# Score products of two heads on the two halves of the matmul array's rows, in a decoder trunk with sparse attention

## The chip, the cores and the metric

One core of a Trainium2 chip runs the whole program. The metric is the device time of one execution in microseconds; a lower one is better. The core's engines run side by side: PE (TensorE, matrix products into the eight PSUM banks), PEld (its weight loads), DVE (VectorE), ACT (ScalarE), POOL (GpSimd) and SP, which here issues nearly all DMAs.

## The reference

Two layers over 512 tokens of width 1024. Each is half a SwiGLU step, a mixer, and half a SwiGLU step. In the mixer, 16 heads of width 64 in 2 key groups attend in three branches; the change touches the scores, `q` times keys:

```python
q = (q * q_scale).reshape(B, T, N_KV_GROUPS, HEADS_PER_GROUP, HEAD_DIM)
# compressed keys (31 of them)
s = einsum('bqghd,bngd->bghqn', qc, k_cmp) - slopes * dist_c
o_cmp = einsum('bghqn,bngd->bqghd', masked_softmax(s, dist_c >= 0), v_cmp)
# selected blocks (all 8 blocks are selected) and the sliding window of 512 keys
s = einsum(qc, ks) - slopes * dist_s;  o_slc = masked_softmax(s, dist_s >= 0) @ vs
s = einsum(qc, kw) - slopes * dist_w;  o_win = masked_softmax(s, mask_w) @ vw
o_nsa = gates[0] * o_cmp + gates[1] * o_slc + gates[2] * o_win
merged = g_pool * (o_pool @ w_branch_pool) + g_attn * (o_nsa @ w_branch_nsa)
x = x + merged @ w_out
```

## The kernel before, in words

Activations lie transposed: a tile has 128 features by 512 tokens. Float32 accuracy comes from splitting each operand into a rounded high part and the rest (`split`, L113: ACT copies, DVE subtracts) and summing three products, high by high, high by low, low by high (`mm3`, L117). Weights come through SP in blocks of 1 MB (`load`, L95), are split a step ahead of use, and each unit of a projection is 24 products of 512 columns (`proj`, L126).

The program is written as a list of steps (`run_steps`, L279); within them nobody writes an engine's order out. A planner takes all instructions with their program order as priority and lays each engine's queue down when the program is built: an instruction goes in when its operands and a free buffer of its tag are there in the plan, and a later one that is ready goes ahead of one that isn't. So the products of projections, transposes and heads stand mixed in PE's queue.

PSUM has eight banks of 512 columns by tag (L34): `mm` 2, `sc` 2, `pt` 3, `pv` 1. The attention of a layer runs over 16 heads:

- `query_unit` (L562) makes the queries of two heads. Each head gets a tile of its own, `q`: its 64 rows hold the high part, the other 64 rows the low part. The keys `KH` hold the high part twice, once in each half; `KL` the low part. So one product of 128 rows gives high by high plus low by high, and a second with `KL` gives high by low (L645, L655): two products a bank.
- `cmp_probs` (L576), once for four heads, scores the 31 compressed keys: eight products of 128 rows (L584) into one `sc` bank.
- `head_probs` (L619): for each of four blocks of 128 queries and each of two branches, the scores of all keys up to the block (128 to 512 columns); DVE adds the distance and takes the minimum (L634), ACT takes the exponential (L636), DVE scales by gate over sum (L660 to L664). In blocks 0 and 1 both branches share a bank; in blocks 2 and 3 each has its own, so a head fills six `sc` banks.
- `head_out` (L666): 20 transposes a head into six `pt` banks (L677), each bank split (ACT, DVE), then 17 products with the values into `pv` (L691); the sum of its halves goes to `o` (L695), a tile in SBUF that holds all heads.

Head h's probabilities are written ahead of head h-1's outputs, and between heads stand "fill" units, the gate projections and later queries (L749). After head 15 `split_out` (L765) splits `o` for the next projection, `branch_nsa` (L783).

Of the kernel before, what the change touches and what calls it, by code (L numbers as in the profile page):

```python
# [17 lines left out]
P = 128  # L18
# [12 lines left out]
OFF_KC, OFF_KS, OFF_KW, OFF_GATE = 1024, 1280, 1536, 1792  # L31
OFF_POOL, OFF_GP, OFF_GA = 1840, 2352, 3376
SLOPES = [float(np.float32(2.0 ** (-(h + 1) / 2))) for h in range(H)]
BANKS = {"mm": 2, "sc": 2, "pt": 3, "pv": 1}  # L34
FF_CHUNKS = ((0, 8), (8, 8), (16, 6))

ROWS = {"ffn1_norm": 0, "mix_norm": 16, "ffn2_norm": 32, "final_norm": 48,
# [14 lines left out]
class Trunk:  # L52
# [416 lines left out]
    def compress_out(self, w2, hid, which):  # L469
        nc = self.nc  # L470
        hs = self.s("hs")[:62, :256]
        nc.scalar.activation(hs, hid[64:126, :256], AF.Copy)
        nc.vector.tensor_add(hs, hid[:62, :256], hs)
        nc.scalar.activation(hs, hs, AF.Gelu_apprx_tanh)
        tp = self.bank("pt")
        for c in range(2):
            nc.tensor.transpose(tp[:, c * 62 : c * 62 + 62], hs[:, c * P : c * P + P],
                                self.ident[:62, :62])
        w2r = self.s("w2r")[:, :128].rearrange("p (c d) -> p c d", c=2)
        nc.sync.dma_start(w2r, w2.rearrange("(c p) d -> p c d", p=P))  # L480
        w2h, w2l = self.pr("w2h"), self.pr("w2l")
        if which == 0:
            hh, hl = self.pr("hh")[:, :124], self.pr("hl")[:, :124]
            self.split(hh, hl, tp[:, :124])
            w2h, w2l = (w[:, :256].rearrange("p (c r d) -> p c r d", c=2, r=2)
                        for w in (w2h, w2l))
            self.split(w2h, w2l, bc(w2r, 2, 2))
            kp = self.bank("pv")
            self.mm3(kp[:, :62], [
                (w2h[:, c].rearrange("p r d -> p (r d)"), w2l[:, c].rearrange("p r d -> p (r d)"),  # L490
                 hh[:, c * 62 : c * 62 + 62], hl[:, c * 62 : c * 62 + 62]) for c in range(2)])
            self.Kc = []
            for g in range(G):
                kc = self.unit("Kc", 2, F32R, "Kc", (P, 2, 224))
                nc.gpsimd.memset(f32(kc), 0.0)
                self.split(kc[:, 0, 96:127], kc[:, 1, 96:127], kp[:, g * NCMP : g * NCMP + NCMP])
                self.Kc.append(kc)
            return
        hh, hl = (self.pr(n).rearrange("p (a j n) -> p a j n", a=4, j=4) for n in ("hh", "hl"))
        nc.gpsimd.memset(f32(hh), 0.0)  # L500
        nc.gpsimd.memset(f32(hl), 0.0)
        src = bc(tp[:, :124].rearrange("p (a n) -> p a n", a=4), 2, 4)
        for a in range(4):
            self.split(hh[:, a, :, :NCMP], hl[:, a, :, :NCMP], src[:, a])
        w2h, w2l = (w[:, :128].rearrange("p (c d) -> p c d", c=2) for w in (w2h, w2l))
        self.split(w2h, w2l, w2r)
        self.Vc = []
        for g in range(G):
            vp = self.bank("pv")
            self.mm3(vp[:, :DH], [  # L510
                (hh[:, 2 * c + g].rearrange("p j n -> p (j n)"),
                 hl[:, 2 * c + g].rearrange("p j n -> p (j n)"), w2h[:, c], w2l[:, c])
                for c in range(2)])
            vm = self.s("vm")[:, :128].rearrange("p (j d) -> p j d", j=2)
            nc.vector.tensor_mul(vm, bc(vp[:, :DH], 1, 2), bc(self.block, 2, DH))
            vc = self.unit("Vc", 2, F32R, "Vc", (P, 2, 2, DH))
            self.split(vc[:, :, 0], vc[:, :, 1], vm)
            self.Vc.append(vc)
# [43 lines left out]
    def query_unit(self, m, w):  # L562


        nc = self.nc
        p = self.proj("mm", w, self.xg)
        qn = self.s("qn")
        nc.vector.scalar_tensor_tensor(qn, p, self.qcol[:, m : m + 1], self.R, ALU.mult, ALU.mult)
        for e in range(2):
            q = self.unit("x", 8, F32R, "q")  # L570
            me, other = slice(e * DH, e * DH + DH), slice(DH - e * DH, 2 * DH - e * DH)
            nc.scalar.activation(q[me], qn[me], AF.Copy)
            nc.vector.tensor_sub(q[other], qn[me], f32(q[me]))
            self.qs[2 * m + e] = q

    def cmp_probs(self, qd):  # L576

# [1 line left out]
        nc = self.nc  # L579
        kc = self.Kc[qd // 2]  # L580
        sp = self.bank("sc")
        for j in range(4):
            for part in range(2):
                nc.tensor.matmul(sp, kc[:, part, 96 - 32 * j : 224 - 32 * j], self.qs[4 * qd + j],  # L584
                                 start=j + part == 0, stop=j == 3 and part == 1)
        st = self.s("st")
        nc.vector.tensor_add(st, sp, self.distc)
        tp = self.bank("pt")
# [27 lines left out]
            nc.vector.tensor_sub(pc[other], tp[me], f32(pc[me]))  # L616
            self.pc[qd].append(pc)

    def head_probs(self, h):  # L619

        nc = self.nc
        g, q = h // 8, self.qs.pop(h)
        m, c = self.sm(8, "m"), self.sm(8, "c")
        probs = self.probs[h] = {}

        def slot():
            i = self.tpos % 16
            self.tpos += 1  # L630
            return self.tbuf[i // 8][:, i % 8]

        def softmax_num(t, sp, i, nk):
            nc.vector.tensor_tensor_reduce(t, sp, self.dist[:, T - nk :], SLOPES[h], 3e38,  # L634
                                           ALU.add, ALU.min, m[:, i : i + 1])
            nc.scalar.activation(t, t, AF.Exp, scale=-1.0, bias=m[:, i : i + 1],  # L636
                                 accum_out=c[:, i : i + 1])

        for qb in range(TB):
            nk = P * (qb + 1)  # L640
            qq = q[:, qb * P : qb * P + P]
            if qb < 2:
                sp = self.bank("sc")[:, : 2 * nk]
                for i, K in enumerate((self.KH[g], self.KL[g])):
                    nc.tensor.matmul(sp, qq, K[:, :, :nk], start=i == 0, stop=i == 1)  # L645
                t2 = slot()[:, : 2 * nk].rearrange("p (r k) -> p r k", r=2)
                s2 = sp.rearrange("p (r k) -> p r k", r=2)
                for br in range(2):
                    softmax_num(t2[:, br], s2[:, br], 2 * qb + br, nk)
                    probs[qb, br] = t2[:, br]  # L650
            else:
                for br in range(2):
                    sp = self.bank("sc")[:, :nk]
                    for i, K in enumerate((self.KH[g], self.KL[g])):
                        nc.tensor.matmul(sp, qq, K[:, br, :nk], start=i == 0, stop=i == 1)  # L655
                    t = slot()[:, :nk]
                    softmax_num(t, sp, 2 * qb + br, nk)
                    probs[qb, br] = t
            ci = c[:, 2 * qb : 2 * qb + 2]
            nc.vector.reciprocal(ci, ci)  # L660
            nc.vector.tensor_mul(ci, ci, self.gates[:, qb, 3 * h + 1 : 3 * h + 3])
            for br in range(2):
                t = probs[qb, br]
                nc.vector.tensor_scalar(t, t, ci[:, br : br + 1], None, ALU.mult)  # L664

    def head_out(self, h):  # L666
        nc = self.nc
# [24 lines left out]
        tmp = self.s("otmp")  # L692
        nc.scalar.activation(tmp[:DH], out[DH:], AF.Copy)
        r = (h % 2) * DH
        nc.vector.tensor_add(self.o[r : r + DH, h // 2], out[:DH], tmp[:DH])  # L695


    def mixer(self, l, on_x):
# [3 lines left out]
        def scratch(name):  # L702
            return self.dr.tile([ND, P, T], F32, tag=f"{name}{l}", name=f"{name}{l}")

        dx, dP, dB, dA = (scratch(n) for n in ("dx", "dP", "dB", "dA"))
        self.dx[l] = dx
        self.qs, self.pc, self.probs, self.delta = {}, {}, {}, {}

# [33 lines left out]
                  bp[2]]  # L742

        def start():
            self.tbuf, self.tpos = [self.big(F32, "tbuf") for _ in range(2)], 0
            self.o = self.big(F32, "o")

        steps += [bp[3], (None, start)]
        fill = [gp[0:1] + q[2:3], gp[1:2] + q[3:4], gp[2:3], gp[3:4],  # L749
# [3 lines left out]
        for h in range(H):  # L753
            if h % 4 == 0:
                steps.append((None, lambda h=h: self.cmp_probs(h // 4)))
            steps.append((None, lambda h=h: self.head_probs(h)))
            if h:
                steps.append((None, lambda h=h: self.head_out(h - 1)))
            steps += fill[h]
        steps.append((None, lambda: self.head_out(H - 1)))  # L760

        oh, merged, streams, nx = [], [], {}, [None] * ND
        box = {}
# [1 line left out]
        def split_out():  # L765
            for k in range(ND):
                hi, lo = self.unit("xg", 16, F32R, "oh"), self.unit("xg", 16, F32R, "ol")
                self.split(hi, lo, self.o[:, k])
                oh.append((hi, lo))
            box["mh"], box["ml"] = self.big(F32R, "mh"), self.big(F32R, "ml")  # L770

# [39 lines left out]
    def run(self):  # L811
# [13 lines left out]
        self.x, self.xg = [], []  # L825
        tps = []
        for d in range(ND):
            tp = self.bank(("mm", "sc", "pt", "mm", "sc", "pt", "pt", "pv")[d])
            for tb in range(TB):
                nc.tensor.transpose(tp[:, tb * P : tb * P + P],  # L830
                                    xin[:, tb, d * P : d * P + P], self.ident)
            self.xg.append(self.gain(tp, ROWS["ffn1_norm"] + d))
            tps.append(tp)
# [81 lines left out]
```

## Time and profile before

| | |
|---|---|
| median of 3 runs | 2397.09 us (2396.93 to 2399.38) |
| profiled execution | 2397.52 us, span 2395.7 us |
| granted TensorE clock over the span | 0.995 |
| busy: DVE, ACT, POOL | 1398.9, 977.4, 51.5 us |
| matmuls | 11042 |
| HBM | 101 GB/s over the span |

The span runs from the first to the last instruction; the execution's time has 1.8 us around it. Busy time of PE counts records that overlap, so the room that a product takes is read from the start of one to the start of the next.

### The profile page before, as it was taken

To read this page: it belongs to the slowest core of one execution; us is meant where nothing else is said; L and a number is where in the kernel's file an instruction comes from. 1 tells how busy PE (TensorE), PEld (TensorE's weight loads), DVE (VectorE), ACT (ScalarE), POOL (GpSimd) and SP (SyncE) were. 2 spreads that over 40 slices of the span, in tenths; PEclk is the share of its full clock that TensorE was granted. 3 is DMA by queue.
4 is the path that set the end of the run, shared out by engine and by line. 5 is a ranking of instruction groups with operands and counts; after the bars stand their busy time and mean duration, and the time that the engine had idled before them with its cause. 6 is when DMAs were issued, how large, how long until landed. Compare 5 with 4: busy or idle time off the path is not lost.

```text
span 2395.7 us, 28552 instructions
## 1 busy us (share of the span) xinstructions
PE 2363.0 (99%) x11042; PEld 1955.6 (82%) x11042; DVE 1398.9 (58%) x2684; ACT 977.4 (41%) x1689; POOL 51.5 (2%) x106
## 2 busy tenths in 40 slices
PE   8999999999999999999999999999999999999998
PEld 6888888778888888888888888887888887888887
DVE  4434346768988544443544443567988975434444
ACT  4222235556666432222332222345666664322222
POOL 1000000000001000000000000000000010000000
PEclk9999999999999999999999999999999999999999
DMA  5323224522124432323223232334222253232321
GB/s 159 104 90 105 89 97 140 158 82 62 58 76 153 138 105 89 101 93 101 92 89 105 89 105 90 119 115 156 71 71 80 71 185 110 88 106 88 106 79 62
DMA packets 226007, 244.24 MB, mean 102 GB/s; under 512 B 8688, under 2 KB 206416, under 8 KB 225872
## 3 DMA queue, kind: packets, MB, share of 16 engines
q1 hardware_dynamic: 225696, 242.37, 31.6%
q8 instruction: 87, 1.43, 0.3%
q14 instruction: 48, 0.39, 0.1%
q10 hardware_dynamic: 176, 0.05, 0.0%
HBM read 223.53 MB, written 18.87 MB: 101 GB/s over the span
## 4 chain that ended last, share of the span: by engine, by line
PE 58%; issue 15%; DVE 1%; POOL 1%; ACT 0%; DMA 0%; POOLq 0%; DVEq 0%; ACTq 0%; SPq 0%
PE ps_mm L122 9%; PE ps_mm L121 9%; PE ps_mm L123 9%; PE ps_pv L691 4%; PE ps_sc L121 3%; PE ps_sc L123 3%; PE ps_sc L122 3%; PE ps_pt L121 3%; PE ps_pt L122 3%; PE ps_pt L123 3%; PE ps_pt L677 3%; PE ps_sc L655 2%; PE ps_sc L645 1%; PE ps_sc L584 0%; DMA bP<-dB 0%
## 5 line engine op out<-in xcount | busy, mean ns | idle before, releaser
L114 ACT ACTIVATE wh<-wr 128x1024 fp32r<-128x1024 f32 (+1 forms) x392 | 408.8, 1043 | 1082.5 <-PE ps_mm L122 399.8
L115 DVE TENSOR_TENSOR wl<-wr,wh 128x1024 fp32r<-128x1024 f32 (+1 forms) x392 | 470.1, 1200 | 78.8 <-ACT wh L114 77.3
L121 PE MATMUL ps_sc<-xh,wh 128*128 128x512 f32 x704 | 276.8, 393 | 2.2 <-ACT x L840 2.2
L123 PE MATMUL ps_sc<-xh,wl 128*128 128x512 f32 x704 | 274.7, 390 | 0.0
L122 PE MATMUL ps_sc<-xl,wh 128*128 128x512 f32 x704 | 274.4, 390 | 0.0
L122 PE MATMUL ps_mm<-act,wh 128*128 128x512 f32 x704 | 274.4, 390 | 0.0
L123 PE MATMUL ps_mm<-act,wl 128*128 128x512 f32 x704 | 273.9, 389 | 0.0
L121 PE MATMUL ps_pt<-xh,wh 128*128 128x512 f32 x704 | 273.9, 389 | 0.0
L122 PE MATMUL ps_pt<-xl,wh 128*128 128x512 f32 x704 | 273.9, 389 | 0.0
L123 PE MATMUL ps_pt<-xh,wl 128*128 128x512 f32 x704 | 273.9, 389 | 0.0
L121 PE MATMUL ps_mm<-act,wh 128*128 128x512 f32 x704 | 273.3, 389 | 0.0
L342 DVE SCALAR_TENSOR_TENSOR x<-ps_mm,x 128x512 f32<-128x512 f32 x96 | 66.4, 692 | 239.7 <-PE ps_mm L123 239.7
L333 DVE TENSOR_TENSOR u<-ps_pt,R 128x512 f32<-128x512 f32 x88 | 60.9, 692 | 245.6 <-PE ps_pt L123 245.6
L121 PE MATMUL ps_mm<-xh,wh 128*128 128x512 f32 x512 | 203.2, 397 | 0.0
L325 DVE TENSOR_TENSOR z<-ps_sc,R 128x512 f32<-128x512 f32 x88 | 60.9, 692 | 242.7 <-PE ps_sc L123 242.6
L123 PE MATMUL ps_mm<-xh,wl 128*128 128x512 f32 x512 | 200.8, 392 | 0.0
L122 PE MATMUL ps_mm<-xl,wh 128*128 128x512 f32 x512 | 200.6, 392 | 0.0
L121 PEld LDWEIGHTS ps_sc<-xh,wh 128*128 128x128 f32 x704 | 132.6, 188 | 30.9 <-ACT x L840 2.6
L636 ACT ACTIVATE tbuf<-tbuf,m 128x128 f32<-128x128 f32 (+3 forms) x256 | 142.2, 556 | 36.2 <-DVE m L634 28.3
L122 PEld LDWEIGHTS ps_sc<-xl,wh 128*128 128x128 f32 x704 | 132.6, 188 | 28.1 <-issue 1.0
L122 PEld LDWEIGHTS ps_mm<-act,wh 128*128 128x128 f32 x704 | 132.2, 188 | 28.5 <-DVE act L115 1.3
L123 PEld LDWEIGHTS ps_sc<-xh,wl 128*128 128x128 f32 x704 | 132.5, 188 | 27.9
(238 smaller groups left out, 3870.7 us busy)
## 6 DMA issues: line engine op xcount, KB each, us to landing
wr<-in_ffn_w_gate_dram SPq DMA_DIRECT2D x44, 1024.0 KB, 5.3
wr<-in_ffn_w_up_dram SPq DMA_DIRECT2D x44, 1024.0 KB, 5.3
wr<-in_w_in_dram SPq DMA_DIRECT2D x34, 1024.0 KB, 5.2
wr<-in_ffn_w_down_dram SPq DMA_DIRECT2D x32, 1024.0 KB, 4.9
wr<-in_ffn_w_down_dram SPq DMA_DIRECT2D x16, 768.0 KB, 4.2
wr<-in_w_branch_nsa_dram SPq DMA_DIRECT2D x8, 1024.0 KB, 5.3
wr<-in_w_out_dram SPq DMA_DIRECT2D x8, 1024.0 KB, 5.3
dx<-x SPq DMA_DIRECT2D x16, 256.0 KB, 2.8
```

Source lines behind the costliest of these rows:

```text
L114: self.nc.scalar.activation(hi, src, AF.Copy)
L115: self.nc.vector.tensor_sub(lo, src, f32(hi))
L121: self.nc.tensor.matmul(out, lh, rh, start=first and i == 0, stop=False)
L122: self.nc.tensor.matmul(out, lh, rl, start=False, stop=False)
L123: self.nc.tensor.matmul(out, ll, rh, start=False, stop=last and i == n - 1)
L325: nc.vector.tensor_mul(z, g, self.R)
L333: nc.vector.tensor_mul(u, up, self.R)
L342: nc.vector.scalar_tensor_tensor(x, o, 0.5, x, ALU.mult, ALU.add)
L636: nc.scalar.activation(t, t, AF.Exp, scale=-1.0, bias=m[:, i : i + 1], accum_out=c[:, i : i + 1])
L655: nc.tensor.matmul(sp, qq, K[:, br, :nk], start=i == 0, stop=i == 1)
L677: nc.tensor.transpose(tp[:, w : w + P], probs[qb, br][:, kb * P : kb * P + P], self.ident)
L691: nc.tensor.matmul(out[:, T - n :], lhsT, rhs, start=i == 0, stop=i == len(ops) - 1)
```

## The change

The two heads of a pair keep their places: head 2m in rows 0 to 63, head 2m+1 in rows 64 to 127 of one high tile and one low tile. The scores of each head are three products of 64 rows, the two heads' written alternately into two `sc` banks. `sc` gets three banks, `pt` two. Probabilities of a pair are made together and scaled at the pair's end (`pair_probs`), into three tiles in place of two; the heads' outputs run one pair behind. As `o` has no room any more, each pair's outputs go to DRAM (`dO`) and `split_out` reads them back, except the last pair's.

```diff
-BANKS = {"mm": 2, "sc": 2, "pt": 3, "pv": 1}
+BANKS = {"mm": 2, "sc": 3, "pt": 2, "pv": 1}
...
-                kc = self.unit("Kc", 2, F32R, "Kc", (P, 2, 224))
+                kc = self.unit("Kc", 2, F32R, "Kc", (P, 2, 192))
...
-                self.split(kc[:, 0, 96:127], kc[:, 1, 96:127], kp[:, g * NCMP : g * NCMP + NCMP])
+                for e in range(2):
+                    rows, c = slice(e * DH, e * DH + DH), 64 + 32 * e
+                    self.split(kc[rows, 0, c : c + NCMP], kc[rows, 1, c : c + NCMP],
+                               kp[rows, g * NCMP : g * NCMP + NCMP])
...
-        for e in range(2):
-            q = self.unit("x", 8, F32R, "q")
-            me, other = slice(e * DH, e * DH + DH), slice(DH - e * DH, 2 * DH - e * DH)
-            nc.scalar.activation(q[me], qn[me], AF.Copy)
-            nc.vector.tensor_sub(q[other], qn[me], f32(q[me]))
-            self.qs[2 * m + e] = q
+        qh, ql = (self.unit("x", 8, F32R, n) for n in ("qh", "ql"))
+        self.split(qh, ql, qn)
+        self.qs[m] = qh, ql
...
-        for j in range(4):
-            for part in range(2):
-                nc.tensor.matmul(sp, kc[:, part, 96 - 32 * j : 224 - 32 * j], self.qs[4 * qd + j],
-                                 start=j + part == 0, stop=j == 3 and part == 1)
+        self.mm3(sp, [(kc[:, 0, 64 - 64 * e : 192 - 64 * e], kc[:, 1, 64 - 64 * e : 192 - 64 * e],
+                       *self.qs[2 * qd + e]) for e in range(2)])
...
+    def pair_probs(self, m):
...
+        def scores(qb, brs):
+            nk = P * (qb + 1)
+            sps = [self.bank("sc")[:, : len(brs) * nk].rearrange("p (r k) -> p r k", r=len(brs))
+                   for _ in range(2)]
+            for i, (q, K) in enumerate(((qh, KH), (qh, KL), (ql, KH))):
+                for j, sp in enumerate(sps):
+                    rows = slice(j * DH, j * DH + DH)
+                    nc.tensor.matmul(sp, q[rows, qb * P : qb * P + P],
+                                     K[rows, brs[0] : brs[-1] + 1, :nk], start=i == 0, stop=i == 2)
+            for r, br in enumerate(brs):
+                i = 2 * qb + br
+                for (h, probs, mi, c), sp in zip(heads, sps):
+                    t = probs[qb, br]
+                    nc.vector.tensor_tensor_reduce(t, sp[:, r], self.dist[:, T - nk :], SLOPES[h],
+                                                   3e38, ALU.add, ALU.min, mi[:, i : i + 1])
+                    nc.scalar.activation(t, t, AF.Exp, scale=-1.0, bias=mi[:, i : i + 1],
+                                         accum_out=c[:, i : i + 1])
         for qb in range(TB):
...
+            for brs in ((0, 1),) if qb < 2 else ((0,), (1,)):
+                scores(qb, brs)
+        for h, probs, _, c in heads:
+            nc.vector.reciprocal(c, c)
+            c3 = c.rearrange("p (b r) -> p b r", r=2)
+            nc.vector.tensor_mul(c3, c3, self.gates[:, :, 3 * h + 1 : 3 * h + 3])
+            for (qb, br), t in probs.items():
+                i = 2 * qb + br
+                nc.vector.tensor_scalar(t, t, c[:, i : i + 1], None, ALU.mult)
...
-        nc.vector.tensor_add(self.o[r : r + DH, h // 2], out[:DH], tmp[:DH])
+        if r == 0:
+            self.o = self.s("o")
+        nc.vector.tensor_add(self.o[r : r + DH], out[:DH], tmp[:DH])
+        if r and h < H - 1:
+            nc.sync.dma_start(self.dO[h // 2], self.o)
...
-            steps.append((None, lambda h=h: self.head_probs(h)))
-            if h:
-                steps.append((None, lambda h=h: self.head_out(h - 1)))
+            if h % 2 == 0:
+                steps.append((None, lambda h=h: self.pair_probs(h // 2)))
+            if h > 1:
+                steps.append((None, lambda h=h: self.head_out(h - 2)))
             steps += fill[h]
-        steps.append((None, lambda: self.head_out(H - 1)))
+        for h in (H - 2, H - 1):
+            steps.append((None, lambda h=h: self.head_out(h)))
...
-                self.split(hi, lo, self.o[:, k])
+                o = self.o
+                if k < ND - 1:
+                    o = self.unit("x", 8, F32, "ob")
+                    nc.sync.dma_start(o, dO[k])
+                self.split(hi, lo, o)
```

## Rows read from the trace of the kernel before

**Rows 1.** The page's busy times: us (share of the span) and instructions.

```profile
PE 2363.0 (99%) x11042; PEld 1955.6 (82%) x11042; DVE 1398.9 (58%) x2684; ACT 977.4 (41%) x1689; POOL 51.5 (2%) x106
```

**Rows 2.** Windows: length, busy us by engine (instructions), clock, DMA share, GB/s.

```profile
622.00:690.00 68.00, 67.71 (x361) 56.06 (x361) 60.12 (x185) 43.75 (x109) 1.05 (x1) 1.00 0.25 78
```

**Rows 3.** Waits of PE's loads, 555 to 757 us: total us, times, longest.

```profile
PEld ps_pv L691 <- ACT ph L114: 2.3, 8, 0.4
```

**Rows 4.** Groups by form: busy us, mean ns | idle before.

```profile
L655 PE MATMUL ps_sc<-KH,q 128*128 128x512 f32 x64 | 25.7, 402 | 0.0
```

**Rows 5.** Timeline of PE, 557 to 587 us: start, us, what.

```profile
557.39 2.04 PE L584 MATMUL ps_sc<-q,Kc 128*128 128x512 f32 x8
...
579.39 0.28 PE L645 MATMUL ps_sc<-KH,q 128*128 128x256 f32 x1
...
579.62 0.40 PE L645 MATMUL ps_sc<-KH,q 128*128 128x512 f32 x1
...
582.41 0.33 PE L655 MATMUL ps_sc<-KH,q 128*128 128x384 f32 x1
...
582.76 0.39 PE L121 MATMUL ps_mm<-xh,wh 128*128 128x512 f32 x1
...
584.61 0.34 PE L655 MATMUL ps_sc<-KH,q 128*128 128x384 f32 x1
...
585.19 0.39 PE L655 MATMUL ps_sc<-KH,q 128*128 128x512 f32 x1
...
585.65 0.39 PE L121 MATMUL ps_mm<-xh,wh 128*128 128x512 f32 x1
...
586.11 0.39 PE L655 MATMUL ps_sc<-KH,q 128*128 128x512 f32 x1
```

**Rows 6.** Timeline, 460 to 461.4 us, around the transposes of L477.

```profile
460.20 0.42 ACT L474 ACTIVATE hs<-hs 62x256 f32<-62x256 f32 x1
...
460.44 0.39 PE L122 MATMUL ps_mm<-xl,wh 128*128 128x512 f32 x1
460.76 0.20 PEld L477 LDWEIGHTS ps_pt<-ident,hs 62*128 62x128 f32 x2 [0.35 <-ACT hs L474]
...
461.03 0.50 PE L123 MATMUL ps_mm<-xh,wl 128*128 128x512 f32 x1
...
461.36 0.40 PE L121 MATMUL ps_mm<-xh,wh 128*128 128x512 f32 x1
```

**Rows 7.** Timeline, 580.7 to 581.4 us: a load that waits for ACT.

```profile
580.72 0.60 ACT L114 ACTIVATE ph<-ps_pt 128x512 fp32r<-128x512 f32 x1
...
581.37 0.19 PEld L691 LDWEIGHTS ps_pv<-ph,V 128*128 128x128 f32 x1 [0.27 <-ACT ph L114]
```

**Rows 8.** Timeline, 28.0 to 28.9 us, around a transpose of 80 rows.

```profile
28.07 0.39 PE L122 MATMUL ps_sc<-xl,wh 128*128 128x512 f32 x1
...
28.53 0.23 PE L169 MATMUL ps_pv<-ident,rows 80*128 80x80 f32 x1
...
28.87 0.39 PE L122 MATMUL ps_sc<-xl,wh 128*128 128x512 f32 x1
```

**Rows 9.** Timeline of PE, 385 to 386.1 us: products of two columns.

```profile
385.20 0.95 PE L243 MATMUL ps_pv<-ones,acc 128*128 128x2 f32 x8
386.01 0.49 PE L121 MATMUL ps_mm<-xh,wh 128*128 128x512 f32 x1
```

**Rows 10.** Groups by form on DVE, over the span.

```profile
L634 DVE CUSTOM_DVE_ANT_0 tbuf<-ps_sc,dist 128x512 f32<-128x512 f32 x64 | 43.5, 680 | 0.5
...
L661 DVE TENSOR_TENSOR c<-c,gates 128x2 f32<-128x2 f32 x128 | 22.3, 174 | 0.1
...
L660 DVE RECIPROCAL c<-c 128x2 f32<-128x2 f32 x128 | 20.5, 160 | 1.6 <-ACT tbuf L636 1.0
```

**Rows 11.** DMA issues (KB each, median us to landing), and a product near the attention's end.

```profile
dA<-z SPq DMA_DIRECT2D x16, 256.0 KB, 4.3
...
748.64 0.48 PE L121 MATMUL ps_mm<-oh,wh 128*128 128x512 f32 x1
```

More of the change, by code (lines that the diff above doesn't have):

```diff
@@ L617, in cmp_probs @@
             self.pc[qd].append(pc)
-    def head_probs(self, h):
+    def pair_probs(self, m):
         nc = self.nc
[L624 to L637, printed above, removed]
-        for qb in range(TB):
[L640 to L664, printed above, removed]
@@ new lines, in pair_probs @@
+        g, (qh, ql) = m // 4, self.qs.pop(m)
+        KH, KL = self.KH[g], self.KL[g]
+        heads = []
+        for j in range(2):
+            h = 2 * m + j
+            probs = self.probs[h] = {}
+            heads.append((h, probs, self.sm(8, "m"), self.sm(8, "c")))
+            for br in range(2):
+                i = 4 * (m % 2) + 2 * j + br
+                chunk = self.tbuf[i // 3][:, i % 3 * 1280 : i % 3 * 1280 + 1280]
+                w = 0
+                for qb in range(TB):
+                    probs[qb, br] = chunk[:, w : w + P * (qb + 1)]
+                    w += P * (qb + 1)
@@ L703, in scratch @@
             return self.dr.tile([ND, P, T], F32, tag=f"{name}{l}", name=f"{name}{l}")
-        dx, dP, dB, dA = (scratch(n) for n in ("dx", "dP", "dB", "dA"))
+        dx, dP, dB, dA, dO = (scratch(n) for n in ("dx", "dP", "dB", "dA", "dO"))
         self.dx[l] = dx
@@ L744, in start @@
         def start():
-            self.tbuf, self.tpos = [self.big(F32, "tbuf") for _ in range(2)], 0
-            self.o = self.big(F32, "o")
+            self.tbuf = [self.big(F32, "tbuf").rearrange("p k t -> p (k t)") for _ in range(3)]
+            self.dO = dO
         steps += [bp[3], (None, start)]
@@ L827, in run @@
         for d in range(ND):
-            tp = self.bank(("mm", "sc", "pt", "mm", "sc", "pt", "pt", "pv")[d])
+            tp = self.bank(("mm", "sc", "pt", "mm", "sc", "pt", "sc", "pv")[d])
             for tb in range(TB):
```

## The prediction

> **What bounds the kernel now.** I read the page's busy times first: the matmul engine is busy for 99% of the span, the next engine for 58% [rows 1]. A stage could still hide another limit, so I cut the attention (about 487 to 757 us, and 1665 to 1936 us in the second layer) into stretches of four heads: there PE is busy for 67.71 of 68 us at full clock, DVE for 60.12 [rows 2]. Busy matmul records overlap, so I then asked what PE's weight loads wait for: over 202 us of attention the longest entry of any engine is 2.3 us [rows 3]. Last I read starts instead of durations from the timeline, because a product's record (402 ns, [rows 4]) is longer than the room it takes: two products of 256 columns take 0.23 us from start to start (579.39 to 579.62), two of 384 take 0.35, two of 512 take 0.46 [rows 5]. So PE streams without a pause here. A microsecond taken from PE's stream is a microsecond of the kernel, and one added is one lost; DVE and ACT have 8 us and more of air in 68.
>
> **The score products.** A head has 12 of them: two of 256 columns, two of 512, four of 384, four of 512. By the spacings above that is 0.23 + 0.46 + 0.70 + 0.92 = 2.31 us, 4.62 us for two heads, 73.9 us for the 16 pairs of both layers. After the change a pair has 36 products of 64 rows with the same column counts, three where one head had two, in 12 bank fillings. The trace of before has no two products side by side on halves of the array, so this is bounded from both sides:
> - One after another: 4.62 x 1.5 = 6.93 us a pair, +37.0 us over 16 pairs.
> - Fully side by side: 3.46 us a pair, -18.5 us.
> - Side by side, but each product with a weight load of its own: eight products of only 2 columns take 0.81 us [rows 9], so a load costs some 0.10 us whatever it multiplies, and two of them 0.21 us, more than a pair of 256 (0.115) or 384 columns (0.175) streams. Then 3 x 0.21 + 3 x 0.23 + 6 x 0.21 + 6 x 0.23 = 3.96 us a pair, -10.5 us.
>
> Which bound holds depends on whether the two halves' products stand next to each other in PE's order. The code writes them alternately, but the order is a planner's: in before each refill of a score bank becomes a run of its own as the bank comes free (579.39, 582.41, 584.61, 585.19 and 586.11 for one head, [rows 5]), with other products between. After the change a filling needs two of three banks. The first finds two free, the next finds one: its first half can go at once, its partner waits until DVE has emptied another. DVE empties one 512-column bank in 0.68 us [rows 10], while the three products of a half take 3 x 0.23 = 0.69 us, so a partner comes late about as often as not. I take half of the products beside their partner: (3.96 + 6.93) / 2 = 5.45 us a pair, +13.2 us; -18.5 and +37.0 are kept for the range.
>
> **Changing between 128 and 64 rows.** The one place of before where PE leaves the 128-row form for 64 or fewer are the two 62-row transposes of L477. They begin 0.32 us after the product ahead of them instead of 0.23, and not for want of data: ACT's tile is ready at 460.62 and the load starts at 460.76, 0.14 us later [rows 6], where a load that really waits for ACT starts 0.05 us after it (580.72 + 0.60, then 581.37, [rows 7]). Behind them the next weights are loaded only when they have ended. From 460.44 to 461.36 it is 0.92 us, 0.46 more than the two 512-column products in it need. A transpose of 80 rows, with no change of form, adds 0.80 - 3 x 0.23 = 0.11 us [rows 8]; two would add 0.22 to 0.24. So the change there and back costs 0.46 - 0.24 = 0.22 us at least, and 0.40 if the two transposes are charged only for their 62 columns. All four places of the trace show the same 0.92. I take the middle, 0.31 us for every run of 64-row products, since a run of score products streams longer than its later loads but pays for the first load and the one after it.
>
> Runs: 6 a pair if all six products of a filling stand together, 12 if each bank is a run. I take 8 (some fillings join, half are split): 128 runs x 0.31 = +39.7 us; the ends are 96 x 0.22 = 21 and 192 x 0.40 = 77 us.
>
> The Trainium skill (TensorE: Matmul & The Clock Gate, Part 3: Packing small matmuls) speaks for the change: products on different row groups run concurrently, a few ns apart, 3.07 times as fast for four groups. By it alone the sum would be that of full overlap, which is the first rival below; no run here shows it.
>
> **Compressed scores.** L584 drops from eight 512-column products to six in each of 8 stages. Eight take 0.235 us each [rows 5]: 16 x 0.235 = -3.8 us. They keep 128 rows.
>
> **Edits that I cost at nothing.** The reciprocal and the gate product now run once a head, not four times: 192 instructions of some 0.17 us [rows 10] leave DVE, and the queries are split in one piece, not two. DVE is not what PE waits for: in the view of [rows 3] the loads wait some 5 us of 202 for DVE and ACT, 14 us over both layers, and PE streams on during most of it. So this gives 0 to -14 us; I take 0. The halves of the compressed keys add some small ACT and DVE instructions well ahead of their use. The transposes lose one of three banks; other products fill in as they do for the scores: 0, at most half of one 0.68 us evacuation a head [rows 10], +11. Probabilities are now scaled at a pair's end, one pair ahead of their transposes; the cover is the fill products. Head outputs leave through SP by 14 stores and come back by 14 loads of 256 KB. A store of that size lands in 4.3 us [rows 11], and two heads lie between the last store and its use, some 9 us of PE (2 x 5632 value columns at 0.23 us per 512, 40 transposes of at least 0.10); uncovered it would be about 7 us a layer. SP waits there only behind issues for later weights. At the tail two heads are left after the last fill instead of one; the next stage's products are already mixed in there (748.64 us, [rows 11]), so 0, at most one head's six splits of 0.68 us, +4 us a layer.
>
> **Sum.** +13.2 + 39.7 - 3.8 = +49.1 us. The profiled execution took 2397.5 us (span 2395.7 and 1.8 around it), 0.4 above the median of the runs; on the median that gives 2446 us.
>
> **Rivals.**
> - *Faster: the halves overlap and the change of form is nearly free.* Then -10.5 to -18.5 - 3.8: 2375 to 2383 us, say 2379. For it: PE is the bound, so saved columns count in full. Against it: the four L477 places. It decides only if a run's price, with 96 runs, falls below (10.5 + 3.8) / 96 = 0.15 us (0.23 with full overlap).
> - *Six together.* Every filling's products stay alternate and overlap, but pay 96 x 0.31 = 29.8: +29.8 - 3.8 - 10.5 to 18.5 gives 2405 to 2413 us. For it: the order written in the code. Against it: one free bank lets one half start alone.
> - *The halves never overlap, so the change does not do what its words say.* +37.0 + 39.7 - 3.8 = +72.9: 2470 us; with the ends for the runs 2451 to 2507. For it: no overlap in the trace. Against it: nothing in the trace either.
>
> **How the numbers follow.** Forecast 0.40 (own range 2420 to 2470), faster rival 0.15, six together 0.23, no overlap 0.22. About 0.2% (5 us) is what a measurement of this kernel can tell from no change. Of the faster rival 0.14 is beyond that; 0.06 (the low end of six together, the high end of the first) is within; 0.80 is slower. The range 2390 to 2490 leaves out most of the faster rival and the top of the last.
>
> **What would show it.** In the changed trace: partner products starting a few ns apart or 0.23 us apart; the number of runs of 64-row products, 96 to 192; the step into a run (0.32 against 0.23 us) and a load that starts only after the run; the attention of a layer some 25 us longer while the FFN stages keep their length. Were runs entered at 0.23 us with loads ahead, the main term would be wrong; a long wait of the branch products for reloaded outputs, or PE idle behind DVE, would be a cost that I left out.

## The result and the profile after

The changed kernel takes 2482.88 us (median of 4 runs, 2480.55 to 2487.14) against 2397.43: a ratio of 1.0361, interval 1.0349 to 1.0374. It is slower by 85 us where the sum gave 49. The profiled execution took 2480.73 us, its span is 2478.8 us, 83.1 longer than before, at a granted clock of 0.992.

PE is still the busy engine, with 176 more products; DVE and ACT have less to do than in [rows 1]:

```profile
PE 2431.8 (98%) x11218; PEld 1953.8 (79%) x11218; DVE 1380.6 (56%) x2480; ACT 963.2 (39%) x1677; POOL 50.9 (2%) x106
```

The windows of the two attentions and the one of [rows 2] (length, then busy us of PE, PEld, DVE, ACT, POOL, clock, DMA share, GB/s) show something new: PE is busy for 65.44 of 68 us where it was for 67.71, and in the two attentions it stands for 9 us each.

```profile
487.00:834.00 347.00, 338.11 (x1683) 251.11 (x1683) 252.94 (x657) 193.44 (x467) 14.88 (x13) 1.00 0.29 95
1707.00:2059.00 352.00, 343.08 (x1683) 255.05 (x1683) 252.35 (x657) 192.79 (x466) 14.37 (x11) 0.98 0.28 94
622.00:690.00 68.00, 65.44 (x331) 46.98 (x330) 48.54 (x128) 36.53 (x96) 1.05 (x1) 1.00 0.24 78
```

What PE's loads wait for, in the stretch of [rows 3] (total us, times, longest): the value products waited 2.3 us for ACT's copies of the transposes, now 15.1, up to 1.3 at a time. The transposes' wait for DVE (1.2 before) and the score loads' wait at the line `issue`, on the step into a run (2.1 before), have grown as well.

```profile
PEld ps_pv L692 <- ACT ph L114: 15.1, 33, 1.3
PEld ps_sc L645 <- issue: 8.6, 33, 0.4
...
PEld ps_pt L678 <- DVE pl L115: 3.9, 10, 0.5
```

The timeline of PE around one whole filling and one half filling, to be read by starts as [rows 5]:

```profile
556.96 0.39 PE L123 MATMUL ps_sc<-qh,Kc 128*128 128x512 f32 x1
557.28 0.39 PE L645 MATMUL ps_sc<-KH,qh 64*128 64x256 f32 x2
557.50 0.28 PE L645 MATMUL ps_sc<-KL,qh 64*128 64x256 f32 x2
557.62 0.28 PE L645 MATMUL ps_sc<-KH,ql 64*128 64x256 f32 x2
557.82 0.50 PE L121 MATMUL ps_mm<-xh,wh 128*128 128x512 f32 x1
558.16 0.40 PE L122 MATMUL ps_mm<-xl,wh 128*128 128x512 f32 x1
...
559.40 0.50 PE L645 MATMUL ps_sc<-KH,qh 64*128 64x512 f32 x1
559.75 0.40 PE L645 MATMUL ps_sc<-KL,qh 64*128 64x512 f32 x1
559.99 0.39 PE L645 MATMUL ps_sc<-KH,ql 64*128 64x512 f32 x1
560.31 0.50 PE L122 MATMUL ps_mm<-xl,wh 128*128 128x512 f32 x1
```

The `x2` are partners on the two halves; these start 3 to 4 ns apart. Into the run goes 0.32 us (556.96 to 557.28) where a product of 512 columns makes room after 0.23. The second step inside is long too (0.22 for 256 columns, then 0.12; 0.35 for 512, then 0.24), so is the last (559.99 to 560.31, 0.32) and the first product behind (557.82 to 558.16, 0.34): about 0.1 us at each of four places. The whole trace has 116 runs of such products, and 174 of 460 products inside runs start sooner behind the one ahead than three quarters of the time that the columns of the one ahead take (I call these early starts).

And this is what the pauses look like, in the same layer, all engines:

```profile
587.97 0.45 PE L692 MATMUL ps_pv<-pc,Vc 128*128 128x512 f32 x1
...
588.25 0.60 PE L678 MATMUL ps_pt<-ident,tbuf 128*128 128x128 f32 x4
...
589.07 0.60 ACT L114 ACTIVATE ph<-ps_pt 128x512 fp32r<-128x512 f32 x1
589.08 0.68 DVE L698 TENSOR_TENSOR o<-ps_pv,otmp 64x512 f32<-64x512 f32 x1 [0.21 <-ACT otmp L694]
...
589.68 0.67 DVE L721 TENSOR_TENSOR z<-ps_mm,R 128x512 f32<-128x512 f32 x1
...
589.91 0.47 PE L692 MATMUL ps_pv<-ph,V 128*128 128x512 f32 x1 [1.05 <-DVE o L698]
...
590.41 0.50 PE L121 MATMUL ps_mm<-xh,wh 128*128 128x512 f32 x1
```

PE has written four transposes (588.25), and the value products that use them stand next in its queue: they wait for ACT's copy (`ph`, ready at 589.67) and for the one `pv` bank, which DVE's sum `o` frees at 589.76. A projection's product comes only at 590.41, when DVE has read `z` out of an `mm` bank. Nothing else stands in the queue to be mixed in, and PE stands for a microsecond. With two transpose banks PE writes few transposes ahead of the value products that use them, so the copy in between comes late; that the banks are the cause is argued here and tried below.

To put sizes on this I measured every start-to-start step of PE from the first compressed product to the last product before the output projection, charged 227 ns for 512 columns (less in proportion) and 109 ns for a transpose, and kept score stretches, with the longer steps into and behind a run, apart from all other pauses. In the kernels with scores of 128 rows the score column is the plain charge; pauses at their score steps stand under other pauses. Us per layer, first and second layer (one number where both agree):

| kernel | attention | scores and runs | other pauses |
|---|---|---|---|
| before | 308.8, 306.9 | 36.3 | 18.0, 16.1 |
| changed | 346.1, 351.2 | 68.5 | 25.1, 30.1 |
| rows64_alone | 336.4, 334.5 | 71.0 | 10.9, 9.1 |
| banks_2_3 | 333.5, 335.2 | 70.5 | 10.5, 12.1 |
| same_half | 344.9, 346.6 | 82.2 | 10.0, 11.7 |
| six_together | 335.9, 335.9 | 56.0 | 27.3, 27.2 |
| pairs_128 | 346.6, 346.9 | 36.3 | 55.8, 56.1 |
| pairs_128_banks_2_3 | 316.7, 319.0 | 36.3 | 25.9, 28.2 |
| before_banks_3_2 | 318.9, 317.6 | 36.3 | 28.1, 26.8 |

Before to changed: scores and runs +64.4 over both layers, compressed scores -3.6, other pauses +21.1, together +82 of the 83 us. The split depends on the column for 128 rows: in the kernel before, the steps of score products, into them and behind them, already hold 6.4 us of pauses a layer. With every step at a score counted as such in both kernels it is 42.8 against 71.1 us a layer, so +57 for scores and runs and +29 for other pauses (22 to 50 over both layers).

### The profile page after: what moved, and what is told of

Same layout as the page of the kernel before. It is cut to its first block, busy times and chain, and to the rows that moved or that the text cites. A ratio compares the mean times of both kernels' runs of the same rounds, so it can differ in the third digit from the quotient of the medians.

```text
span 2478.8 us, 28755 instructions
## 1 busy us (share of the span) xinstructions
PE 2431.8 (98%) x11218; PEld 1953.8 (79%) x11218; DVE 1380.6 (56%) x2480; ACT 963.2 (39%) x1677; POOL 50.9 (2%) x106
## 4 chain that ended last, share of the span: by engine, by line
PE 78%; issue 15%; DVE 3%; ACT 1%; DMA 1%; POOL 1%; POOLq 0%; SPq 0%; DVEq 0%; ACTq 0%
PE ps_mm L121 12%; PE ps_mm L123 12%; PE ps_mm L122 12%; PE ps_sc L121 5%; PE ps_sc L123 5%; PE ps_sc L122 5%; PE ps_pt L123 5%; PE ps_pt L121 5%; PE ps_pt L122 5%; PE ps_pv L692 4%; PE ps_sc L645 4%; PE ps_pt L678 3%; DMA bP<-dB 1%; PE ps_sc L461 0%; ACT ph L114 0%
## 5 line engine op out<-in xcount | busy, mean ns | idle before, releaser
L122 PEld LDWEIGHTS ps_mm<-act,wh 128*128 128x128 f32 x704 | 132.1, 188 | 28.8 <-DVE act L115 1.3
L122 PEld LDWEIGHTS ps_pt<-xl,wh 128*128 128x128 f32 x704 | 132.1, 188 | 27.7
```

The source lines that it names most:

```text
L122: self.nc.tensor.matmul(out, lh, rl, start=False, stop=False)
```

## The experiments

Theory: runs of 64-row products cost what the change loses. Rivals: the pair order or the banks do. The kernels shared runs of the kernel before, 2396.6 to 2398.8 us. Lines are those of the changed kernel unless said otherwise.

**The change of form alone** (rows64_alone). Kernel before, each head's scores from its own 64 rows, two products a bank; the low part of the queries is left out.

```diff
-            qq = q[:, qb * P : qb * P + P]
+            me = slice(h % 2 * DH, h % 2 * DH + DH)
+            qq = q[me, qb * P : qb * P + P]
...
-  nc.tensor.matmul(sp, qq, K[:, br, :nk], start=i == 0, stop=i == 1)
+  nc.tensor.matmul(sp, qq, K[me, br, :nk], start=i == 0, stop=i == 1)
```

> The kernel before in its own order, the scores taken from 64 rows of queries and keys: two products a bank as before, with the low part of the queries left out of the scores (the sum high by high plus high by low remains). Same 384 products, same columns, 174 runs of 64-row products in PE's queue. Theory (each run pays the change of form, 0.41 us as read off the changed kernel): 174 x 0.41 = +71 us, near 2468 us. Rival (the change of form is nearly free, the loss of the changed kernel lies in its third product and its order): within 5 us of before.

Measured: 2450.96 us (2448.19 to 2455.26), ratio 1.0235 (1.0214 to 1.0256). With the same columns, 174 runs cost 54 us: less than the theory's 71, far from the rival's limit of 5. An attention grew by 27.6 us, 0.32 us for each of its 87 runs. By the table the score stretches grew by 34.7, 0.40 a run, and 7 us of other pauses went away; with score steps counted alike it is 31, 0.35 a run, and 3 us.

**The pair order without 64 rows** (pairs_128). Changed kernel with the queries, the two products of 128 rows a bank and the compressed scores of before.

```diff
...
-  for i, (q, K) in enumerate(((qh, KH), (qh, KL), (ql, KH))):
-      for j, sp in enumerate(sps):
+  for i, K in enumerate((KH, KL)):
+      for q, sp in zip(qs, sps):
...
```

> The changed kernel with the scores, queries and compressed scores of before (two products of 128 rows a head); pairs, three score banks, two transpose banks, head outputs through DRAM stay. Theory (the 21 us of waits in the changed attention come from 64-row runs that last longer than the planner thought): within 8 us of before. Rival (the pair order with two transpose banks makes the waits by itself): +15 to +25 us. Second rival (the way through DRAM costs at the tail): +5 to +14 us, seen between the last head's output and the next stage.

Measured: 2476.85 us (2470.65 to 2481.61), ratio 1.0335 (1.0305 to 1.0365). My theory fell here, and the rivals' sizes too: without one 64-row product the rest of the change costs 80 us, nearly as much as the whole change. PE stands for 21 of 347 us in the first attention, and the transposes wait for DVE, in one place 2.7 us (the rows: the attention's window, the waits from 487 to 806 us, where the change has 15.9 and 7.6 in place of 20.2 and 17.5, and the timeline there):

```profile
487.00:834.00 347.00, 325.69 (x1595) 257.42 (x1594) 254.97 (x662) 195.49 (x469) 15.90 (x13) 0.97 0.29 95
```

```profile
PEld ps_pv L696 <- ACT ph L114: 20.2, 42, 1.3
PEld ps_pt L682 <- DVE pl L115: 17.5, 29, 2.7
```

```profile
573.58 2.45 DVE L669 TENSOR_SCALAR tbuf<-tbuf,c 128x128 f32<-128x128 f32 x8
...
575.95 0.55 DVE L115 TENSOR_TENSOR pl<-ps_pt,ph 128x384 fp32r<-128x384 f32 x1
...
576.55 0.51 PEld L682 LDWEIGHTS ps_pt<-ident,tbuf 128*128 128x128 f32 x3 [2.67 <-DVE pl L115]
```

Eight scalings of a head stand on DVE ahead of the split that would free a transpose bank, and with two banks there is no other to write. After this pause the granted clock is 0.50:

```profile
575.20:581.90 6.70, 5.02 (x17) 3.80 (x18) 4.52 (x13) 2.45 (x8) 0.00 (x0) 0.50 0.45 153
```

That happens three times in each attention. The products in these six stretches, 41 us long together, take 14.5 us by the charges above, so about 14 of the 80 us are the halved clock.

**The banks back** (banks_2_3). Changed kernel with two score and three transpose banks; outside the attention one tile of the input's transposes moves to the tag that has the bank.

```diff
-BANKS = {"mm": 2, "sc": 3, "pt": 2, "pv": 1}
+BANKS = {"mm": 2, "sc": 2, "pt": 3, "pv": 1}
...
```

> The changed kernel with two score banks and three transpose banks, as before had them. 128 runs of 64-row products instead of 116, 60 of them all six of a filling. Theory (the price is per run, overlap is by the order): +5 us for 12 more runs, some -10 us for more products beside their partner, waits about as they are: 2470 to 2485 us. Rival (the third transpose bank was what the heads waited for): the 21 us of waits go too, near 2458 us.

Measured: 2454.09 us (2450.4 to 2458.53), ratio 1.0247 (1.0225 to 1.0269): 28.8 us less than the change, with more runs (128): the rival. By the table scores and runs cost 2 us a layer more and the other pauses fell from 55 to 23 us over both layers; with score steps counted alike, scores and runs are the same and other pauses fell from 50 to 22, what they were before. In the stretch of [rows 3] the wait of the value products for ACT fell from 15.1 to 3.4 us:

```profile
PEld ps_pv L692 <- ACT ph L114: 3.4, 8, 0.7
```

**Whole fillings** (six_together). Both banks of a filling are one tile of two banks, there are three transpose banks, and the users of the score banks elsewhere are moved.

```diff
-BANKS = {"mm": 2, "sc": 3, "pt": 2, "pv": 1}
+BANKS = {"mm": 2, "sc": 1, "pt": 3, "pv": 1}
...
+    def two(self):
+        return self.ps.tile([P, 2, T], F32, tag="sc", bufs=1, name="ps_sc")
...
```

> The changed kernel with both halves' score banks made one buffer of two banks (three transpose banks; the first half-step's gates and one compressed product moved to other banks so that this fits): 92 of 100 runs hold all six products of a filling. Theory: 100 x 0.41 = +41 us for the runs, -10.5 us for products side by side at the price of their loads, -3.8 us for the compressed scores: 2424 us, up to 2445 us where the waits of the changed kernel stay. Rival (no price per run): -14 us, near 2383 us. Rival (halves do not overlap): near 2470 us.

Measured: 2466.14 us (2459.48 to 2468.36), ratio 1.0292 (1.0269 to 1.0315). The theory's 2424 to 2445 missed; the rival without overlap has the number (2470) but not the cause, as the rows under same_half show. There are 100 runs, 92 of them of six, and the scores cost 14.5 us a layer less than in banks_2_3. But other pauses are 16 us a layer more, and of the 15.6 us by which its span is longer than that of banks_2_3 only 3.1 lie in the attentions: some 12 us are lost in the other stages, 9.6 of them ahead of the first attention. That projections there had used the two banks one by one is the likely reason; it is not shown. What the runs give is lost in waits, which this edit adds by itself.

**The bank swap with 128 rows, from both sides** (pairs_128_banks_2_3 and before_banks_3_2). The same line of `BANKS`, in pairs_128 and, the other way round, in the kernel before.

> The pair order and the way through DRAM with the 128-row scores of before, now with two score and three transpose banks. Theory now (the changed attention is held at 346 us a layer by two transpose banks, with 64-row scores and with 128-row scores alike): with the third bank back PE's stream is the bound again, 2390 to 2405 us. Rival (the order by pairs, or the outputs' way through DRAM, makes the waits): above 2430 us.

> The kernel before with three score and two transpose banks, nothing else changed. Theory (two transpose banks hold the heads back by themselves): +20 to +80 us. Rival (they do so only with the pair order, where a whole pair's score evacuations stand in DVE's queue ahead of a head's splits): within 10 us of before.

Measured: 2417.76 us (2411.11 to 2424.41), ratio 1.0086 (1.0062 to 1.011), and 2420.33 us (2417.84 to 2426.76), ratio 1.011 (1.0091 to 1.0129). So the swap is worth 24 us in the old order, 59 in the pair order with 128 rows, and 29 with 64 rows. It always moves a score bank and a transpose bank together; that the transpose bank is what counts is read from the waits, no run changes one tag alone. My number for the first missed: the pair order, with the way through DRAM, still costs 21 us. Within the pair order, 64 rows in place of 128 cost 36 us with three transpose banks and 6 with two.

**Head outputs through DRAM** (through_dram_alone). Kernel before, with `dO`, its stores and its loads.

```diff
-        nc.vector.tensor_add(self.o[r : r + DH, h // 2], out[:DH], tmp[:DH])
+        nc.vector.tensor_add(self.o[r : r + DH], out[:DH], tmp[:DH])
+        if r and h < H - 1:
+            nc.sync.dma_start(self.dO[h // 2], self.o)
...
```

> The kernel before with the heads' outputs stored to DRAM pair by pair and read back ahead of the next projection, nothing else changed. Theory: within 5 us of before, as two heads or more lie between a store and its use. Rival: +5 to +14 us, the wait standing between the last head and the next stage.

Measured: 2400.43 us (2394.82 to 2405.99, 10 runs), ratio 1.0017 (1.0004 to 1.0031): 1 to 7 us, and its profiled attentions are as long as before (308.2 and 307.8). In the changed kernel the DMAs land sooner than the 4.3 us of [rows 11]:

```profile
dO<-o SPq DMA_DIRECT2D x14, 256.0 KB, 2.0
ob<-dO SPq DMA_DIRECT2D x14, 256.0 KB, 2.7
```

**The order as written** (not_alternate). banks_2_3 with a bank's three products together, one head after the other.

```diff
-  for i, (q, K) in enumerate(((qh, KH), (qh, KL), (ql, KH))):
-      for j, sp in enumerate(sps):
+  for j, sp in enumerate(sps):
+      for i, (q, K) in enumerate(((qh, KH), (qh, KL), (ql, KH))):
```

> The changed kernel with two score and three transpose banks (2454 us), a filling's products written head after head instead of alternately: the same 128 runs, 60 of them whole fillings, but hardly a product beside its partner. Theory (the overlap is worth (6.93 - 3.96) / 6 = 0.50 us a whole filling): 60 x 0.50 = +30 us on 2454, so 2475 to 2495 us. Rival (the overlap is worth nothing, the streams are bound by loads or waits): 2450 to 2460 us.

Measured: 2452.15 us (2449.57 to 2454.69), ratio 1.0239 (1.0223 to 1.0254), the same as banks_2_3. That doesn't say that alternating is worth nothing, for the edit changed little in PE's queue: of the 60 whole fillings of banks_2_3, written alternately, the planner had laid only 6 alternately, 12 in part, and 42 head after head; in not_alternate all 60 stand head after head. What the trace does show is that products on different halves overlap even then. PE's queue holds, at one place:

```
rows 0-63    L645 MATMUL ps_sc<-KH,qh 128x384
rows 0-63    L645 MATMUL ps_sc<-KL,qh 128x384
rows 0-63    L645 MATMUL ps_sc<-KH,ql 128x384
rows 64-127  L645 MATMUL ps_sc<-KH,qh 128x384
rows 64-127  L645 MATMUL ps_sc<-KL,qh 128x384
rows 64-127  L645 MATMUL ps_sc<-KH,ql 128x384
all rows     L692 MATMUL ps_pv<-ph,V 128x512
```

and the timeline of the same products reads:

```profile
607.37 0.52 PE L645 MATMUL ps_sc<-KH,qh 64*128 64x384 f32 x2
607.65 0.41 PE L645 MATMUL ps_sc<-KL,qh 64*128 64x384 f32 x2
607.83 0.41 PE L645 MATMUL ps_sc<-KH,ql 64*128 64x384 f32 x2
608.16 0.50 PE L692 MATMUL ps_pv<-ph,V 128*128 128x512 f32 x1
```

The second head's first product starts 0.08 us after the first head's first, ahead of two products that stand before it in the queue. Of 60 such runs of six only 12 start in the order of the queue.

**No overlap at all** (same_half). banks_2_3 with both heads' scores from rows 0 to 63.

```diff
-                    rows = slice(j * DH, j * DH + DH)
+                    rows = slice(0, DH)
```

> The changed kernel with two score banks and three transpose banks, in which both heads of a pair read rows 0 to 63 of queries and keys, so that the scores of an odd head are those of the even one: as many products of 64 rows, the same columns, the same 128 runs of them, but none can stand beside its partner. Theory (the halves overlap, and that is worth columns): against the same kernel with its halves, 2454 us, the score stretches grow from 57.7 us a layer to the 67 us that 288 products one after another need with the longer first and last step of 58 runs: +19 us, 2466 to 2484 us. Rival (the two halves' records lie beside each other, but the array gives no time back): 2449 to 2459 us.

Measured: 2476.11 us (2472.53 to 2480.27), ratio 1.0327 (1.0306 to 1.0349), 22 us above banks_2_3 and inside the theory's range. All 576 products start in the order of the queue, and none starts early by the measure above. Six products of 384 columns, here and (second fence) in banks_2_3, where the two halves are used:

```profile
607.42 0.44 PE L645 MATMUL ps_sc<-KH,qh 64*128 64x384 f32 x1
607.70 0.33 PE L645 MATMUL ps_sc<-KL,qh 64*128 64x384 f32 x1
607.87 0.34 PE L645 MATMUL ps_sc<-KH,qh 64*128 64x384 f32 x1
608.05 0.34 PE L645 MATMUL ps_sc<-KL,qh 64*128 64x384 f32 x1
608.24 0.51 PE L645 MATMUL ps_sc<-KH,ql 64*128 64x384 f32 x2
608.68 0.66 PE L678 MATMUL ps_pt<-ident,tbuf 128*128 128x128 f32 x4
```

```profile
604.58 0.66 PE L645 MATMUL ps_sc<-KH,qh 64*128 64x384 f32 x2
604.86 0.33 PE L645 MATMUL ps_sc<-KL,qh 64*128 64x384 f32 x1
605.03 0.33 PE L645 MATMUL ps_sc<-KH,ql 64*128 64x384 f32 x1
605.08 0.33 PE L645 MATMUL ps_sc<-KL,qh 64*128 64x384 f32 x1
605.25 0.34 PE L645 MATMUL ps_sc<-KH,ql 64*128 64x384 f32 x1
605.51 0.55 PE L678 MATMUL ps_pt<-ident,tbuf 128*128 128x128 f32 x3
```

1.26 us against 0.93, though in the second fence too the queue has one head after the other. Where the two heads alternate in the queue, as in the 92 whole fillings of six_together, it is 0.72:

```profile
617.05 0.44 PE L653 MATMUL ps_sc<-KH,qh 64*128 64x384 f32 x2
617.33 0.34 PE L653 MATMUL ps_sc<-KL,qh 64*128 64x384 f32 x2
617.50 0.34 PE L653 MATMUL ps_sc<-KH,ql 64*128 64x384 f32 x2
617.77 0.44 PE L686 MATMUL ps_pt<-ident,tbuf 128*128 128x128 f32 x2
```

All 32 of that size there take 0.72 or 0.73 us; the 20 that stand head after head in banks_2_3 take 0.73 to 1.37. So alternating in the queue brings the whole overlap and the other order a part of it, by place. Against banks_2_3 the score stretches of same_half are 11.7 us a layer longer, the other pauses the same.

**Scaling at once** (pairs_128_scale_at_once). pairs_128_banks_2_3 with the reciprocal, gates and scaling inside the loop over blocks, as before.

```diff
         for qb in range(TB):
...
+            for h, probs, _, c in heads:
+                ci = c[:, 2 * qb : 2 * qb + 2]
+                nc.vector.reciprocal(ci, ci)
...
+                    nc.vector.tensor_scalar(t, t, ci[:, br : br + 1], None, ALU.mult)
```

> The pair order with scores of 128 rows, two score banks and three transpose banks (2417.8 us, 20 above the kernel before), with each probability scaled as soon as its block of queries is done, as before, and not at the pair's end. Theory (the scaling at the pair's end makes the transposes late): at least half of the 20 us come back, 2408 us or less. Rival (the order itself: the scores of two heads in one piece, after which the planner has transposes and value products of two heads with too little else to mix in): within 5 us of 2418.

Measured: 2416.02 us (2411.52 to 2418.7), ratio 1.0073 (1.0055 to 1.0091): the rival. With three transpose banks the scaling at the pair's end costs nothing that shows; what the pair order's 21 us with 128 rows are beyond that stays open. With two banks, where the row at 573.58 above has the scalings ahead of the split, it was not tried.

## Why the prediction was right in sign and short in size

The sign and the chain to it held: PE is the bound, a run of 64-row products costs more than the halves give back. The size did not: 2482.88 us is inside 2390 to 2490 but above the forecast's own range of 2420 to 2470: the sum has 49 of the 85 us. Step by step:

- **What bounds the kernel.** Held, but only for the kernel before. I took "PE streams without a pause" over into the changed one.
- **Columns, +13.2 with half of the products beside their partner.** The number held, in part by luck. One after another 1.5 x 36.3 us a layer is +36 in all; same_half shows that overlap gives back 11.7 us a layer with 160 early starts, and the change has 174: an estimate of +36 - 25 = +11. Of the reasons one was half right, that partners must stand next to each other in the queue: that brings the whole overlap (0.72 us above), but not_alternate shows PE taking the other half's product ahead. And the price of a pair side by side was too high: pairs of 256 columns step by 0.12 us (557.50 to 557.62) and of 384 by 0.17 (617.33 to 617.50), not by the 0.21 of two loads.
- **Change of form, 128 runs x 0.31 = +39.7.** The number of runs was near (116). The price was low: 64.4 - 11 = 53 us over 116 runs is 0.46 us, or 0.40, my upper end, with score steps counted alike (57 - 11 = 46 us). The transposes of L477 on which I read the price [rows 6] leave out the longer second step inside a run. In rows64_alone, with no third product and no pair order, it is 0.35 to 0.40 in the stretches and 0.32 in the time.
- **Compressed scores, -3.8.** Held by count: eight products a layer fewer, -3.6 at 0.227 us.
- **"The transposes lose one of three banks; other products fill in as they do for the scores: 0, at most half of one 0.68 us evacuation a head [rows 10], +11."** This is the step that failed. Other pauses grew by 21 us by the table and by 29 with score steps counted alike, and with the banks back 29 us are gone. Other products do not fill in: the value products wait for the same copies, and at 588.25 to 590.41 above no projection's product stood in PE's queue before them. Of the three kernels of the table that have two transpose banks, each has at least 10 us more of other pauses a layer than its twin with three.
- **DVE relief 0, DRAM way 0, tail 0.** The first two held: DVE is 18 us less busy and no gain shows; the DRAM way is 1 to 7 us alone. Outside the two attentions the span grew by 1.5 us. The tail was not tried by itself.
- **Scaling at the pair's end, covered by the fill products.** It held with three transpose banks. With two, the 2.7 us wait in pairs_128 has the scalings in front of it.

Of the rivals, "halves never overlap" had the nearest number (2470) for a wrong reason: partners start a few ns apart, and same_half, where none overlap, is 22 us slower than its twin. "Six together" was run, and lost to waits what its runs saved. The faster rival would have needed a run under 0.15 us. With the old banks the kernel takes 2454 us, 8 us from the forecast: the sum fits that kernel, in which the lent bank plays no part. None of the versions beats the kernel before.

## What to carry to other kernels

When an engine is 99% busy, a buffer taken from a stage beside the change is not free just because that stage hardly waits now: try the lent buffer by itself, in one line, before anything else. Price a change of the array's form by the whole passage, the step in, the second step, the step out and the first product after, times the number of runs that the queue will really have. The order written in the code is not the order in the queue: read the queue before you believe an experiment on order. A cost that shows in one stage can be partly paid by pauses elsewhere, and two causes that each stall the same engine can add up to more or to less than their sum (here +24 for the banks and +21 for the order made +80 together, some 14 of them at a halved clock).

## What the runs showed of the hardware

A run of 64-row products among 128-row ones cost 0.35 to 0.46 us in its stretch here, by the way of counting, at four places of about 0.1 us; in kernel time it was 0.32 us (rows64_alone). The Trainium skill (TensorEngine Tiling (Array Packing), Key Properties) says that changing the tiling mode drains the engine; the longer steps into and out of a run agree with that, the longer second step, inside the run, is not explained by it.

Products on the two row halves start out of the order of the queue: 48 of the 60 runs of six in not_alternate. The Trainium skill (TensorE: Matmul & The Clock Gate, Part 3: Packing small matmuls) has row groups running concurrently, which the partners 3 to 4 ns apart confirm, and matmuls starting strictly in the order of the queue, which those 48 do not. With all products on one half (same_half) none leaves the order. The measurement decides.

A pause can cost twice. In the changed kernel's second layer the value product below starts after 1.06 us in which PE stood, and from 1811.79 on the products behind it take 0.42 to 0.43 us from start to start instead of 0.23. The windows of 1 us show the granted clock at 0.50 there, the lower of the two levels (1.2 GHz), and at 1.00 again from 1815:

```profile
1810.69 0.58 PE L692 MATMUL ps_pv<-ph,V 128*128 128x512 f32 x1 [1.06 <-DVE o L698]
1811.19 0.80 PE L121 MATMUL ps_mm<-xh,wh 128*128 128x512 f32 x1
1811.79 0.63 PE L122 MATMUL ps_mm<-xl,wh 128*128 128x512 f32 x1
1812.21 0.63 PE L123 MATMUL ps_mm<-xh,wl 128*128 128x512 f32 x1
1812.64 0.63 PE L121 MATMUL ps_mm<-xh,wh 128*128 128x512 f32 x1
```

```profile
1812.00:1813.00 1.00, 1.00 (x3) 0.78 (x3) 0.90 (x2) 0.46 (x1) 0.00 (x0) 0.50 0.69 260
```

The second attention, at 0.98 against 1.00 over its window, is 5 us longer than the first, and its other pauses in the table are 5 us more: three such stretches lie in it, with 4.8 us of work by the charges above, and none in the first behind its start. That a pause brings the lower clock each time is not shown; the pauses of the first attention, like the one at 588.25, did not.
